# Attention items of a hybrid decoder block: scores before fillers, and splits moved into the last items

## The chip, the cores and the metric

The kernel runs on one core of one Trainium2 chip, as one program that computes a whole decoder layer. The metric is the device time of one execution in microseconds (us). A time is given as the median of several runs; the profile shows one execution.

TensorE (PE) multiplies, VectorE (DVE) and ScalarE (ACT) do the elementwise work and the reductions, GpSimd (POOL) takes some of it, and SyncE (SP) issues nearly all DMAs. Each engine works through its own instructions in order and waits for the others by semaphores.

## The reference

The layer runs an SSD branch and a differential-attention branch in parallel, merges them by gates, and puts a gated feed-forward part behind. The change touches the attention branch and the gate product that is woven into it:

```python
for i in range(seq // Q_BLOCK):                      # 8 blocks of 128 queries
    q0, q1 = i * Q_BLOCK, (i + 1) * Q_BLOCK
    s = jnp.einsum('bhqd,bhkd->bhqk', q[:, :, q0:q1], k[:, :, :q1]) * scale
    p = jax.nn.softmax(jnp.where(mask, s, -jnp.inf), axis=-1)
    p = p.reshape(bsz, DA_HEADS, 2, Q_BLOCK, q1)
    attn = p[:, :, 0] - lam * p[:, :, 1]             # 8 heads, two softmaxes each
    outs.append(jnp.einsum('bhqk,bhkd->bhqd', attn, v[:, :, :q1]))
o = rms_norm(jnp.concatenate(outs, axis=2), subln_w) * (1.0 - lam_init)
...
gate_ssd, gate_att = jnp.split(jax.nn.sigmoid(gates), N_BRANCH, axis=-1)
merged = gate_ssd * (y_ssd @ w_ssd_o) + gate_att * (y_att @ w_attn_o)
```

Everything is float32. The kernel multiplies in a reduced format and keeps the precision by splitting an operand into a high and a low part and adding three products.

## The kernel before, in words

The attention stage works through 64 items, `items[t] = (j, i)`: head `j` of 8, and within it query block `i` of 8, which sees `i + 1` blocks of 128 keys. An item with `i < 4` is short: both softmaxes fit into one PSUM tile, so `scores(t, 0)` does both. With `i >= 4` it is long, and `scores(t, 0)` and `scores(t, 1)` each fill a tile. The score tiles come from `ps_mm`, which has two buffers, so a tile can be written when the exponentials of the tile two before it are done.

For each item: `scores` on PE (L1624, L1625), `maxima` on DVE (mask and row maximum: L1652 and L1653 for short items, L1658 for long ones), `exps` on ACT (L1667 and L1670, with row sums), `probs` on DVE (a reciprocal L1678, a coefficient L1679, and the difference of the two softmaxes L1680), `transposes` on PE with a copy on ACT (L1688, L1689), and `values` on PE (L1699). The work is software-pipelined by hand: the loop turn of item `t` issues scores of `t + 1` and `t + 2`, probabilities of `t + 1`, transposes of `t` and values of `t - 1`. The order on PE, DVE, ACT and POOL is the order in which the code issues; the order on SP is left to a scheduler.

Between these, `fill(n)` puts `n` steps of an independent product on PE: the attention half of the gate weights against the normalised input (`dense_stream`). A step is three matmuls of 512 columns (L1578 to L1580). Eight steps finish one half of a block in PSUM; then a tanh on ACT (L1583) empties the bank into `gev`, and only then can the next step write, since there is one bank. There are 8 x 2 x 8 = 128 steps in all: `NFIRST` ahead of the items, `nfill` spread over the items by `share`, and `NLAST` = 20 behind them, the tail. `fill` carries steps that it does not do over to the next call in `owed`. The splits of the next weight block (`highs` on ACT, L1553; `lows` on DVE, L1550) are handed out one at a time by `one`.

Every four items the outputs of a group are normalised: `norm_o` copies them (ACT, L1706), squares them on POOL (L1707) and returns two closures. `first` sums on DVE and takes the power on POOL (L1710 to L1713, L146), `second` multiplies by the row factor (DVE L1716) and scales the outputs on POOL (L1717). Then `out_o` transposes and writes them to DRAM (`atd`).

These outputs must be read back and split into high and low (`oT`) for the product with `w_attn_o` (`ao`). `att_in` loads half a head into a staging tile `stg` (SP, L1744); `att_split` splits it: the high part on ACT (L101), the low part on DVE (L102), and asks for the next load. There are 14 such parts, two staging tiles of two halves each, four loads asked for at item 56, and the 14 splits stand in the tail beside the 20 fillers. Three DVE sums and five loads for the adaptive norm (`ada_load`, `adas`) stand in the tail too. The tiles come from a list of 43 slots (`Slots`): `get` takes the one that was freed first.

Of the kernel before, what the change touches and what calls it, by code (L numbers as in the profile page):

```python
# [17 lines left out]
P = 128  # L18
D = 1024
S = 1024  # L20
HALF = 512
# [43 lines left out]
def kernel(ctx: ExitStack, tc: tile.TileContext, a: dict, out: bass.AP, dbg=None):  # L65
# [1528 lines left out]
            SP.dma_start(vt[b][:, kt, :], vd[kt][:, j * P : (j + 1) * P])  # L1594

    stream = dense_stream()
    owed = n_step = 0

    def fill(n):
        nonlocal owed, n_step  # L1600
        n, owed = n + owed, 0
        for m in range(n):
            if m and n_step % KD == 0:
                owed = n - m
                return
            next(stream, None)
            n_step += 1

    items = [(j, i) for j in range(8) for i in range(8)]

# [129 lines left out]
    def att_in():  # L1740
        nonlocal n_in
        if n_in < len(parts):
            k, half = parts[n_in]
            SP.dma_start(stg[n_in // 2 % 2][:, n_in % 2, :], atd[k][:, half * HALF : (half + 1) * HALF])  # L1744
            n_in += 1

    def att_split():
        nonlocal n_att
        if n_att < len(parts):
            k, half = parts[n_att]  # L1750
            st = stg[n_att // 2 % 2][:, n_att % 2, :]
            oT[k][half] = new_hl(f"oT{k}_{half}")
            split(oT[k][half][:, 0, :], oT[k][half][:, 1, :], st)
            n_att += 1
            att_in()

# [9 lines left out]
            hi, lo = w_ao[j] = [wp.tile([P, KD, P], F32R, tag=f"w{n}", name=f"wao{j}_{n}", bufs=4) for n in ("hi", "lo")]  # L1766
            split(hi, lo, raw_ao.pop(j))

    NFIRST, NLAST = 6, 20
    nfill = len(blocks) * 2 * KD - NFIRST - NLAST  # L1770
    share = [2, 2, 2, 2, 2, 1, 1, 1]
    load_heads(0)
    done = 0
    with tc.manual_schedule(engines={EN.PE, EN.DVE, EN.Activation, EN.Pool}):
        fill(2)
        scores(0, 0)
        scores(1, 0)
        maxima(0, 0)
        maxima(1, 0)
        exps(0, 0)  # L1780
        exps(1, 0)
        probs(0)
        fill(4)
        norm, pend = [], None
        for t, (j, i) in enumerate(items):
            quota = (j * sum(share) + sum(share[: i + 1])) * nfill // (8 * sum(share)) - done
            done += quota
            f1 = (quota + 1) // 2
            if long_(t + 1):
                scores(t + 1, 1)  # L1790
            fill(f1)
            scores(t + 2, 0)
            fill(quota - f1)
            if long_(t + 1):
                maxima(t + 1, 1)
                exps(t + 1, 1)
            transposes(t, 0)
            if i >= 4:
                transposes(t, 4)
            if t > 0:  # L1800
                values(t - 1)
            maxima(t + 2, 0)
            if i % 4 in (1, 2) and norm:
                norm.pop(0)()
            else:
                one(lows)
            probs(t + 1)
            exps(t + 2, 0)
            if i % 4 == 3 and pend is not None:
                out_o(*pend)  # L1810
                pend = None
            if i % 4 == 0 and t > 0:
                jj, ii = items[t - 1]
                pend = jj, ii // 4
                norm = norm_o(*pend)
            else:
                one(highs)
            if t == 56:
                SL.put(*qst[0], *kst[0], *klo[0], vt[0])
                stg = [SL.get(f"stg{i}", F32, (P, 2, HALF)) for i in range(2)]  # L1820
                for _ in range(4):
                    att_in()
            if j < 7 and i == 1:
                load_heads(j + 1)
        values(len(items) - 1)
        pend = items[-1][0], 1
        norm = norm_o(*pend)
        SL.put(*pts[0], *qst[1], *kst[1], *klo[1], *pts[1], vt[1], *aTs)
        srow2, adas, ada0 = SL.get("srow2"), [SL.get(f"adas{i}") for i in range(5)], n_ada
        for n in range(NLAST):  # L1830
            if n == 4:
                SP.dma_start(srow2, crowd.broadcast_to([P, D]))
            elif n > 4 and n % 2 == 0 and n < 16:
                ada_load()
            if 14 < n < 18:
                ada_sum(False, True)
            if n in (4, 7):
                norm.pop(0)()
            if n == 14:
                out_o(*pend)  # L1840
            if n == 1:
                fetch_ao(0)
            fill(1)
            if n == NLAST - 1:
                fill(0)
            if n < len(parts):
                att_split()
            if n == 13:
                split_ao(0)
        assert n_att == len(parts) and not highs and not lows and n_step == 2 * KD * len(blocks)  # L1850
        SL.put(osb, gev, mstrip, *stg)
        for k in range(KD):
            SL.put(*hT[k])


        mT = [[None] * 2 for _ in range(KD)]
        wo = [[None] * 4 for _ in range(2)]
        fbs = [h * KF + k for k in range(KF) for h in range(2)]

        wsd = [[dp.tile([P, 2, HALF], F32, tag=f"wsd{m}_{i}", name=f"wsd{m}_{i}") for i in range(2)] for m in range(3)]  # L1860

        def early_load(m):
            ra, rb = [SL.get(f"ws{m}_{i}", F32, (P, 2, HALF)) for i in range(2)]
            for r_, b in ((ra, fbs[m]), (rb, NFF + fbs[m])):
                SP.dma_start(r_.rearrange("p h c -> p (h c)"), a["w_up"][b])
            return ra, rb

        def early_sums(m, ra, rb):
            a11, a12, a21, a22 = ra[:, 0], ra[:, 1], rb[:, 0], rb[:, 1]
            V.tensor_tensor(a22, a21, a22, op=ALU.add)  # L1870
            V.tensor_tensor(a21, a11, a21, op=ALU.subtract)
            V.tensor_tensor(a11, a22, a11, op=ALU.subtract)
            V.tensor_tensor(a12, a12, a11, op=ALU.subtract)
            for i, (x_, y_) in enumerate(((a11, a22), (a21, a12))):
                G.dma_start(wsd[m][i][:, 0], x_)
                G.dma_start(wsd[m][i][:, 1], y_)
            SL.put(ra, rb)

        adas += [SL.get(f"adas{i}") for i in range(5, 8)]
        for _ in range(3):  # L1880
            ada_load()
        gth = SL.get("gth2")
        mst = SL.get("mst")
        mt = SL.get("mt")
        fetch_ao(1)
        ws_raw, wo_raw = deque(), deque()

        def wo_load(kp):
            if kp < 4:
                wo_raw.append(SL.get(f"wo1_{kp}_raw", F32, (P, 2, HALF)))  # L1890
                SP.dma_start(wo_raw[-1], a["w_out"][2 * kp * P : (2 * kp + 2) * P, HALF:].rearrange("(k p) c -> p k c", p=P))

        for j in range(KD):
            w = w_ao.pop(j)
            ps = ps_mm(f"ao{j}")
            SP.dma_start(gth, gad[j])
            SP.dma_start(mst, msd[j])
            block_half(ps[:, 0, :], w, oT, 0)
            split_ao(j + 1)
            fetch_ao(j + 2)  # L1900
            if j < 5:
                for _ in range((4, 1, 1, 1, 3)[j]):
                    ada_sum(False, True)
            if j == 0:
                for _ in range(5):
                    ada_load()
            elif j == 4:
                for r in (2, 3):
                    ada_row(r)
                SL.put(srow2, *adas[1:])  # L1910
            elif j == 6:
                ada_turn(3, adas[0][:KD, :P])
                SL.put(adas[0])
            if j < 3:
                ws_raw.append(early_load(j))
            if 0 < j < 4:
                early_sums(j - 1, *ws_raw.popleft())
            if j == 3:
                wo_load(0)
                wo_load(1)  # L1920
            elif j > 3:
                kp = j - 4
                wo[1][kp] = (new_hl(f"wo1_{kp}_hi"), new_hl(f"wo1_{kp}_lo"))
                raw = wo_raw.popleft()
                split(*wo[1][kp], raw)
                SL.put(raw)
                wo_load(kp + 2)
            block_half(ps[:, 1, :], w, oT, 1)
            for half in range(2):
                hsl = slice(half * HALF, (half + 1) * HALF)  # L1930
                V.scalar_tensor_tensor(mt[:, hsl], gth[:, hsl], 1.0, ps[:, half, :], op0=ALU.add, op1=ALU.mult)
                V.tensor_tensor(mt[:, hsl], mt[:, hsl], mst[:, hsl], op=ALU.add)
                mT[j][half] = new_hl(f"mT{j}_{half}")
                split(mT[j][half][:, 0, :], mT[j][half][:, 1, :], mt[:, hsl])
# [729 lines left out]
```

## Time and profile before

| | |
|---|---|
| median of 3 runs | 1814.69 us (1813.57 to 1814.9) |
| the profiled execution, its own time | 1814.9 us |
| its span, first to last instruction | 1813.1 us |
| PE busy | 1766.1 us, 97% |
| DVE busy | 1347.0 us, 74% |
| ACT busy | 918.0 us, 51% |
| POOL busy | 175.9 us, 10% |
| mean granted TensorE clock | 0.997 |
| attention stage, from the first filler to the first `ao` matmul | 697.9 to 993.4 us |

A row of the timeline reads: start, duration, engine, line, operation, output and inputs by name, shapes, count, and in brackets how long the engine had been idle and what ended that. Matmuls are pipelined: a row of 512 columns is shown 0.39 us long, though the next may start much sooner, so pitch is read from start to start. A row of waits reads: who waited for whom, microseconds in all, times, the longest. A row of the stretches reads: from and to, length, then busy time and instruction count of PE, weight load, DVE, ACT and POOL, then the granted clock, the DMA share and GB/s.

### The profile page before, as it was taken

The page shows a single profiled execution, that of the slowest core. Times are in us where ns is not written, and L with a number is a line of the kernel's source. Part 1 is how long each engine was busy: PE and PEld are TensorE (multiplying, and loading weights), DVE is VectorE, ACT ScalarE, POOL GpSimd, SP SyncE. Part 2 cuts the span into 40 slices and gives each one's busy share as a digit, 9 for nine tenths or more (in the row PEclk, how much of TensorE's full clock was granted, in tenths as well). Part 3 has the DMA queues.
Part 4 walks back from the last instruction along what each step waited for, and adds up shares of the span by engine and source line. Part 5 has one row for each costly group of instructions (what it writes and reads, how often), then busy time and mean ns, then how long its engine had stood idle before and what let it go on. Part 6 is the DMA issues. An engine that isn't in the chain of part 4 may idle for free.

```text
span 1813.1 us, 23867 instructions
## 1 busy us (share of the span) xinstructions
PE 1766.1 (97%) x8563; PEld 1459.4 (80%) x8563; DVE 1347.0 (74%) x2048; ACT 918.0 (51%) x1642; POOL 175.9 (10%) x183
## 2 busy tenths in 40 slices
PE   7999999999999999999998999999999999999998
PEld 4788888888778888888886888888888888888887
DVE  7887568865767786778776776679898888875545
ACT  7554345456765313666665132655554544554532
POOL 0000000002551200121121103100000000000001
PEclk9999999999999999999999999999999999999999
DMA  9465643365767798665635879313232223378754
GB/s 375 189 205 165 184 140 104 116 243 171 228 203 250 171 376 224 198 169 143 168 127 177 322 257 376 129 55 122 91 134 105 96 103 110 120 238 295 247 161 158
DMA packets 148330, 337.29 MB, mean 186 GB/s; under 512 B 15570, under 2 KB 50290, under 8 KB 148212
## 3 DMA queue, kind: packets, MB, share of 16 engines
q1 hardware_dynamic: 145012, 325.28, 54.6%
q0 software_dynamic: 3200, 10.49, 1.5%
q8 instruction: 67, 1.10, 0.3%
q14 instruction: 51, 0.42, 0.1%
HBM read 240.46 MB, written 95.25 MB: 185 GB/s over the span
## 4 chain that ended last, share of the span: by engine, by line
PE 48%; DVE 11%; DMA 6%; ACT 4%; issue 3%; POOL 1%; SPq 0%; DVEq 0%; POOLq 0%; ACTq 0%
PE upx L2029 4%; PE upx L2028 4%; PE upx L2030 4%; PE o L1699 2%; DMA gst<-gld_s 2%; PE upy L2029 2%; PE upy L2028 2%; PE upy L2030 2%; PE mix L2102 2%; PE mix L2104 2%; PE mix L2103 2%; PE so L123 2%; PE so L125 2%; PE so L124 2%; PE sc L1625 1%
## 5 line engine op out<-in xcount | busy, mean ns | idle before, releaser
L2028 PE MATMUL upx<-t,wu_t 128*128 128x512 f32 x264 | 103.1, 391 | 0.5 <-DVE cv L2488 0.4
L2029 PE MATMUL upx<-t,wu_t 128*128 128x512 f32 x264 | 102.8, 390 | 0.2 <-DVE t L2159 0.2
L2030 PE MATMUL upx<-t,wu_t 128*128 128x512 f32 x264 | 102.7, 389 | 0.0
L2002 ACT ACTIVATE wu_t<-sab 128x512 fp32r<-128x512 f32 x57 | 34.1, 627 | 127.6 <-DVE sab L2019 127.6
L102 DVE TENSOR_TENSOR g_lo<-gst,g_hi 128x1024 fp32r<-128x1024 f32 (+1 forms) x42 | 47.5, 1134 | 50.5 <-ACT g_hi L101 50.5
L1670 ACT ACTIVATE p<-sc,nmx 128x640 f32<-128x640 f32 (+3 forms) x64 | 61.5, 961 | 36.8 <-DVE nmx L1658 34.2
L1658 DVE CUSTOM_DVE_ANT_0 sc<-sc,mstrip 128x640 f32<-128x640 f32 (+3 forms) x64 | 65.5, 1032 | 13.5 <-PE sc L1625 13.1
L101 ACT ACTIVATE g_hi<-gst 128x1024 fp32r<-128x1024 f32 (+1 forms) x42 | 41.5, 988 | 66.4 <-DMA gst<-gld_s 38.8
L1699 PE MATMUL o<-vt,aT 128*128 128x128 f32 x576 | 74.8, 275 | 0.0
L1699 PEld LDWEIGHTS o<-vt,aT 128*128 128x128 f32 x576 | 69.3, 192 | 0.6
L1624 PE MATMUL sc<-kst,qst 128*128 128x512 f32 (+3 forms) x192 | 67.0, 354 | 0.0
L2547 POOL TENSOR_TENSOR rsf<-rsf,nhalf 128x1 f32<-128x1 f32 x8 | 5.2, 656 | 624.2 <-DVE rsf L2546 624.2
L1689 ACT COPY aT<-at 128x512 f32<-128x512 f32 (+2 forms) x96 | 42.7, 480 | 44.2 <-PE at L1688 44.2
L1625 PE MATMUL sc<-klo,qst 128*128 128x512 f32 (+3 forms) x192 | 64.0, 342 | 0.0
L546 PE MATMUL xx<-xt,xw_t 128*128 128x512 f32 x156 | 60.9, 390 | 0.0
L2046 DVE SCALAR_TENSOR_TENSOR ug<-cg,vec,ug 128x1023 f32<-128x1023 f32 (+1 forms) x44 | 56.3, 1280 | 6.1 <-ACT ug L2045 5.3
L548 PE MATMUL xx<-xt,xw_t 128*128 128x512 f32 x156 | 60.7, 389 | 0.0
L547 PE MATMUL xx<-xt,xw_t 128*128 128x512 f32 x156 | 60.7, 389 | 0.0
L1688 PE MATMUL at<-ident,p 128*128 128x128 f32 x288 | 42.5, 274 | 17.5 <-DVE p L1680 14.2
L2006 DVE TENSOR_TENSOR wu_t<-sab,wu_t 128x512 fp32r<-128x512 f32 x57 | 39.3, 690 | 26.6 <-ACT wu_t L2002 26.6
L2028 PEld LDWEIGHTS upx<-t,wu_t 128*128 128x128 f32 x264 | 49.6, 188 | 11.8 <-DVE cv L2488 1.3
L2029 PEld LDWEIGHTS upx<-t,wu_t 128*128 128x128 f32 x264 | 49.6, 188 | 10.5 <-DVE t L2159 0.5
(579 smaller groups left out, 5728.4 us busy)
## 6 DMA issues: line engine op xcount, KB each, us to landing
adas<-in_w_ada SPq DMA_DIRECT2D x32, 512.0 KB
wuf<-in_w_up SPq DMA_DIRECT2D x22, 512.0 KB
gld_s<-gsum SPq DMA_DIRECT2D x22, 512.0 KB
gst<-gld_s SPq DMA_DIRECT2D x20, 512.0 KB
wdt_raw<-wtd SPq DMA_DIRECT2D x20, 512.0 KB
wuv<-in_w_up SPq DMA_DIRECT2D x19, 512.0 KB
gld_a<-ug SPq DMA_DIRECT2D x33, 256.0 KB
adat<-in_w_ada SPq DMA_DIRECT2D x16, 512.0 KB
```

Of the source, the lines that this page charges most:

```text
L546: T.matmul(o, wh, xh_, start=(k == 0 and first), stop=False, skip_group_check=not first)
L547: T.matmul(o, wh, xl_, start=False, stop=False, skip_group_check=not first)
L548: T.matmul(o, wl, xh_, start=False, stop=(k == KH - 1), skip_group_check=not first)
L1624: T.matmul(sc, qs_[s][:, tsl], ks_[s][:, n0:n1], start=True, stop=False)
L1625: T.matmul(sc, qs_[s][:, tsl], kl[s][:, n0:n1], start=False, stop=True)
L1658: V.tensor_tensor_reduce(out=sc, in0=sc, in1=strip, scale=-1.0, scalar=BIG, op0=ALU.add, op1=ALU.min, accum_out=nmx[bq][s][:, 0:1])
L1670: A.activation(p.rearrange("p (h t) -> p h t", h=2) if i == 4 else p, sc, AF.Exp, scale=-1.0, bias=nmx[bq][s][:, 0:1], accum_out=ssum[bq][ ...
L1699: T.matmul(po_of[j, grp][:, qi, :], aTs[t % 2][:, kt // 4, kt % 4, :], vt[j % 2][:, kt, :], start=(kt == 0), stop=(kt == i))
L2028: T.matmul(out_, wh, xh_, start=(k == 0 and first), stop=False, skip_group_check=not first)
L2029: T.matmul(out_, wh, xl_, start=False, stop=False, skip_group_check=not first)
L2030: T.matmul(out_, wl, xh_, start=False, stop=(k == end), skip_group_check=not first)
L2046: V.scalar_tensor_tensor(u[:, d:], c_[:, : S - d], fw[:, 2 - d : 3 - d], u[:, d:], op0=ALU.mult, op1=ALU.add)
```

## The change

`fill` gets a flag `ended`: once a half of a block is finished, no call does another step until the flag is cleared, which happens once per item (and once per filler of the tail). Before, only the rest of the same call was put off.

If the next item is short, the scores of `t + 2` come first and the whole quota of fillers behind them. Before, half of the quota came first in every item.

`NFIRST` goes from 6 to 8, and `share` gives item 2 of a head one filler less and item 5 one more.

`first` stays ahead of the probabilities at item 5, but goes behind them at item 1; `second` goes behind them at items 2 and 6.

In the turns of items 58 to 63 one split each is done, its low part on POOL. There are three staging tiles, six loads are asked for at item 56, and so eight of the 14 splits are left for the tail. `mstrip`, the mask of the long items, gives back its slot before the tail and not behind it.

```diff
@@ -1594,17 +1594,18 @@
     stream = dense_stream()
-    owed = n_step = 0
+    owed, n_step, ended = 0, 0, False
 
     def fill(n):
-        nonlocal owed, n_step
+        nonlocal owed, n_step, ended
         n, owed = n + owed, 0
         for m in range(n):
-            if m and n_step % KD == 0:
+            if ended:
                 owed = n - m
                 return
             next(stream, None)
             n_step += 1
+            ended = n_step % KD == 0
@@ -1741,16 +1742,18 @@
-            SP.dma_start(stg[n_in // 2 % 2][:, n_in % 2, :], atd[k][:, half * HALF : (half + 1) * HALF])
+            SP.dma_start(stg[n_in // 2 % 3][:, n_in % 2, :], atd[k][:, half * HALF : (half + 1) * HALF])
             n_in += 1
 
-    def att_split():
+    def att_split(eng=V):
         nonlocal n_att
         if n_att < len(parts):
             k, half = parts[n_att]
-            st = stg[n_att // 2 % 2][:, n_att % 2, :]
+            st = stg[n_att // 2 % 3][:, n_att % 2, :]
             oT[k][half] = new_hl(f"oT{k}_{half}")
-            split(oT[k][half][:, 0, :], oT[k][half][:, 1, :], st)
+            o = oT[k][half]
+            A.activation(o[:, 0, :], st, AF.Copy)
+            eng.tensor_tensor(o[:, 1, :], st, o[:, 0, :].bitcast(F32), op=ALU.subtract)
             n_att += 1
             att_in()
@@ -1766,9 +1769,9 @@
-    NFIRST, NLAST = 6, 20
+    NFIRST, NLAST = 8, 20
     nfill = len(blocks) * 2 * KD - NFIRST - NLAST
-    share = [2, 2, 2, 2, 2, 1, 1, 1]
+    share = [2, 2, 1, 2, 2, 2, 1, 1]
@@ -1780,17 +1783,21 @@
-        fill(4)
+        fill(6)
         norm, pend = [], None
         for t, (j, i) in enumerate(items):
             quota = (j * sum(share) + sum(share[: i + 1])) * nfill // (8 * sum(share)) - done
             done += quota
             f1 = (quota + 1) // 2
+            ended = False
             if long_(t + 1):
                 scores(t + 1, 1)
-            fill(f1)
-            scores(t + 2, 0)
-            fill(quota - f1)
+                fill(f1)
+                scores(t + 2, 0)
+                fill(quota - f1)
+            else:
+                scores(t + 2, 0)
+                fill(quota)
@@ -1800,11 +1807,13 @@
             maxima(t + 2, 0)
-            if i % 4 in (1, 2) and norm:
+            if i % 4 in (0, 3):
+                one(lows)
+            elif i == 5:
                 norm.pop(0)()
-            else:
-                one(lows)
             probs(t + 1)
+            if norm and i != 5:
+                norm.pop(0)()
             exps(t + 2, 0)
@@ -1817,15 +1826,17 @@
             if t == 56:
                 SL.put(*qst[0], *kst[0], *klo[0], vt[0])
-                stg = [SL.get(f"stg{i}", F32, (P, 2, HALF)) for i in range(2)]
-                for _ in range(4):
+                stg = [SL.get(f"stg{i}", F32, (P, 2, HALF)) for i in range(3)]
+                for _ in range(6):
                     att_in()
+            if 57 < t:
+                att_split(G)
...
-        SL.put(*pts[0], *qst[1], *kst[1], *klo[1], *pts[1], vt[1], *aTs)
+        SL.put(*pts[0], *qst[1], *kst[1], *klo[1], *pts[1], vt[1], *aTs, mstrip)
...
+            ended = False
             fill(1)
             if n == NLAST - 1:
-                fill(0)
+                while owed:
+                    ended = False
+                    fill(0)
...
-        SL.put(osb, gev, mstrip, *stg)
+        SL.put(osb, gev, *stg)
```

## The prediction

> **What bounds the kernel now.** I read the page's first line, then the busy time by stretch, then the waits inside the attention stretch, then the rows in order of time around them.
>
> ```profile
> span 1813.1 us, 23867 instructions
> ...
> 697.90:970.80 272.90, 253.05 (x1632) 222.84 (x1631) 211.12 (x478) 171.02 (x410) 46.33 (x45) 0.99 0.56 160
> 970.80:993.30 22.50, 16.69 (x67) 13.12 (x66) 14.21 (x23) 12.12 (x20) 3.62 (x3) 0.85 0.75 242
> 993.30:1081.60 88.30, 87.77 (x386) 71.92 (x386) 68.19 (x100) 22.85 (x29) 6.65 (x12) 1.00 0.78 279
> ...
> PE at L1688 <- DVE p L1680: 14.2, 20, 1.3
> PE gap L1578 <- ACT gev L1583: 8.2, 4, 5.1
> PE at L1688 <- ACT ga_hi L1553: 3.3, 3, 1.1
> ```
>
> In the stretches (PE busy first, clock and DMA share near the end) PE is nearly full after 993.3, but lacks 20 us in the items and 6 us in the 20-filler tail, where the mean clock is 0.85. So PE sets the end, and what it waits for in these two stretches is what the change can win. The waits name it: 17.5 us in 23 waits at the transposes (the three charged to ACT stand at the same place and have the same length), 8.2 us at a filler that needs its PSUM bank emptied by the tanh (L1583).
>
> A pass 512 wide starts 0.23 us after the one before (below, 993.12 and 993.35), so I measure a loss from start to start; it is about 0.16 longer than the wait printed. By that measure each head loses 2.78 us: 0.51 at the 7-wide transposes (A), 1.27 at the 8-wide (B), 1.0 at the 3-wide one of the next head (C).
>
> ```profile
> 824.40 0.39 PE L1625 MATMUL sc<-klo,qst 128*128 128x512 f32 x1
> 824.94 1.23 DVE L1658 CUSTOM_DVE_ANT_0 sc<-sc,mstrip 128x1024 f32<-128x1024 f32 x1 [0.42 <-PE sc L1625]
> 828.93 0.95 PE L1688 MATMUL at<-ident,p 128*128 128x128 f32 x7 [0.35 <-DVE p L1680]
> 830.08 1.11 ACT L1670 ACTIVATE p<-sc,nmx 128x1024 f32<-128x1024 f32 x1 [1.26 <-DVE nmx L1658]
> 830.98 1.04 POOL L1717 TENSOR_TENSOR osb<-osb,sqt 128x512 f32<-128x512 f32 x1 [2.58 <-DVE sqt L1716]
> 831.52 0.52 DVE L1679 SCALAR_TENSOR_TENSOR coef<-ssum,nlam,rsm 128x1 f32<-128x1 f32 x1
> 833.50 0.74 PE L1688 MATMUL at<-ident,p 128*128 128x128 f32 x5 [1.11 <-DVE p L1680]
> ...
> 841.09 0.39 PE L1625 MATMUL sc<-klo,qst 128*128 128x512 f32 x1
> 843.12 0.68 DVE L1710 TENSOR_REDUCE sso<-osb 128x4 f32<-128x512 f32 x1
> 844.18 0.16 DVE L1678 RECIPROCAL rsm<-ssum 128x2 f32<-128x2 f32 x1
> 845.19 0.82 DVE L1658 CUSTOM_DVE_ANT_0 sc<-sc,mstrip 128x640 f32<-128x640 f32 x1
> 845.42 0.52 PE L1688 MATMUL at<-ident,p 128*128 128x128 f32 x3 [0.85 <-DVE p L1680]
> 845.93 0.15 DVE L1716 TENSOR_TENSOR sqt<-sqt,rsm 128x4 f32<-128x4 f32 x1
> 846.20 1.10 DVE L1679 SCALAR_TENSOR_TENSOR coef<-ssum,nlam,rsm 128x1 f32<-128x1 f32 x1
> 846.40 0.80 ACT L1670 ACTIVATE p<-sc,nmx 128x640 f32<-128x640 f32 x1
> 847.50 0.39 PE L1624 MATMUL sc<-kst,qst 128*128 128x512 f32 x1
> ```
>
> The first group is one chain: PE ends item 7's first scores at 824.63, DVE runs without a break through maximum, `first`, probabilities of item 6, the next maximum; ACT takes the exponential, DVE the last probabilities, PE goes on at 833.50: 8.87 us. PE's own work in between is 8.87 less A and B, 7.09.
>
> **The change part by part.** *Shares and the place of `norm`.* Item 5 of a head gets a second filler, item 2 loses one. Three passes are 3 x 0.2275 = 0.68 us, and at item 5 the second filler stands behind the scores that start the chain: PE's work becomes 7.77. The chain gets shorter by 0.30: `second` now stands behind the probabilities, so L1717 on POOL no longer runs beside L1679, which took 0.52 there and 1.10 at 846.20 and ended with it. A is gone, B keeps 8.57 - 7.77 = 0.80: a gain of 0.98 a head. Putting item 7's scores ahead of its filler costs nothing as long as item 7's exponential (830.08 + 1.11 = 831.19) leaves the bank first. PE, which began that item at 830.98, will come 0.68 - 0.51 later, at 831.15: a tie, worth 0.1 at most if lost.
>
> *Scores first where the next item is short.* From the end of item 3's scores (841.32) PE has two fillers and one, as before one and two; PE's arrival at the 3-wide transposes hardly moves against the chain. `first` (843.12 to the next reciprocal at 844.18, 1.06 us) now comes after the probabilities, so 0.85 of waiting vanishes. What is late next: `first` still stands ahead of item 4's maximum, that maximum ends at 845.93, its exponential can start some 0.2 later (here 846.40, behind a copy of transposes that were late) and takes 0.80, and the next scores (here 847.50) need that PSUM bank. PE would arrive at 841.32 + 5.07 (four fillers 2.73, scores 0.59 twice, transposes and values 1.16) = 846.39, and waits to 846.95. Of C's 1.0 I count 0.45.
>
> ```profile
> 961.96 0.96 PE L1688 MATMUL at<-ident,p 128*128 128x128 f32 x7 [0.75 <-DVE p L1680]
> 966.23 1.06 PE L1688 MATMUL at<-ident,p 128*128 128x128 f32 x8 [1.28 <-DVE p L1680]
> ```
>
> The last head has no scores ahead and only the extra filler helps: 0.68. With the three small waits for tanh (0.68 together, removed by `ended`) the items give 7 x 0.98 + 0.68 + 7 x 0.45 + 0.68 = **11.4**. Ends: the 21.9 that all losses add up to, and 3, if DVE's chain swallows nearly all.
>
> *Start: eight fillers ahead, so that the first half ends there; `ended`.*
>
> ```profile
> 707.69 0.59 ACT L1583 ACTIVATE gev<-gap 128x512 f32<-128x512 f32 x1
> 708.34 0.50 PE L1578 MATMUL gap<-b,w_gate_hi 128*128 128x512 f32 x1 [2.12 <-ACT gev L1583]
> 709.98 0.63 PE L1579 MATMUL gap<-b,w_gate_hi 128*128 128x512 f32 x1
> 713.12 0.49 PE L1688 MATMUL at<-ident,p 128*128 128x128 f32 x3
> ```
>
> PE stands 2.12 + 0.16 us for a tanh that ACT takes late. Then its passes are slow: from 709.98 to 713.12 it needs 3.14 us for five passes of 512 and four of 320, which at 0.23 and 0.15 are 1.7; with the edges some 1.6 is lost. Both go: 3.9. In their place I put 0.15 (tanh against one set of scores) and 0.45 for a wait as in C, which this head did not have: **3.3**; ends 1.5 and 3.9. [...]
>
> *Six splits inside the last items, third staging tile.*
>
> ```profile
> 974.52 0.50 PE L1578 MATMUL gap<-hT,ga_hi 128*128 128x512 f32 x1 [0.69 <-ACT gev L1583]
> 982.84 1.16 ACT L101 ACTIVATE oT<-stg 128x512 fp32r<-128x512 f32 x2 [1.41 <-DMA stg<-atd]
> 984.75 0.58 ACT L1583 ACTIVATE gev<-gap 128x512 f32<-128x512 f32 x1
> 985.38 0.80 PE L1578 MATMUL gap<-b,ga_hi 128*128 128x512 f32 x1 [5.12 <-ACT gev L1583]
> 988.86 1.29 ACT L101 ACTIVATE oT<-stg 128x512 fp32r<-128x512 f32 x2 [1.83 <-DMA stg<-atd]
> 989.68 0.40 PE L1580 MATMUL gap<-b,ga_lo 128*128 128x512 f32 x1
> 993.12 0.39 PE L1580 MATMUL gap<-hT,ga_lo 128*128 128x512 f32 x1
> 993.35 0.39 PE L123 MATMUL ao<-oT,wao_hi 128*128 128x512 f32 x1
> ```
>
> In the tail PE's twelfth filler is done at 980.1, but its tanh is queued on ACT behind splits that wait for staged loads: 5.12 + 0.16 lost; from 985.38 to 989.68 it then needs 4.3 us for eight passes and four transposes of 128, about 2.3: 2.0 more. With eight splits left, six of them loaded long before, ACT is through by about 978, and the second bank costs what the first costs now, 0.69 + 0.15: 5.28 + 2.0 - 0.84 = **6.4**; ends 4 and 7.
>
> ```profile
> L101 ACT ACTIVATE oT<-stg 128x512 fp32r<-128x512 f32 x14 | 8.5, 628 | 8.5 <-DMA stg<-atd 7.7 <-DMA ws<-in_w_up 0.7
> L1707 POOL TENSOR_TENSOR osb<-osb 128x512 f32<-128x512 f32 x16 | 16.7, 1041 | 167.6 <-ACT osb L1706 167.6
> ...
> 926.85 1.91 SPq L561 DMA_DIRECT2D adas<-in_w_ada  x4
> ```
>
> The six splits cost 0.63 us each on ACT, behind an exponential whose successor still waits for DVE (the 1.26 idle at 830.08 covers 0.63), and about 1.04 each on POOL, idle there; uncovered they would cost 3.8 on ACT. POOL's subtraction runs while DVE takes maxima from PSUM and should be over before the next L1679; if each caught one as at 846.20, 6 x 0.88 = 5.3. [...] On SP the staged loads move ahead of the tail; the five `adas` loads, four of them at 926.85 to 928.8 now, lose their tiles to the early splits and must wait for those of items 61 to 63, behind 962. They are read by DVE after the fifteenth tail filler, some 20 us later, and land where ten staged loads were: nothing.
>
> *Afterwards.* PE hardly waits from 993.3 on, so all of it should carry to the end; the next stretch, at a DMA share of 0.78, gets it 6 us sooner and may give back up to 5. I take nothing.
>
> **Sum.** 11.4 + 3.3 + 6.4 = 21.1 against the profiled execution's own 1814.9 us (span 1813.1 and 1.8 around it; the runs' median is 0.2 below): **1793.8**.
>
> **The rivals.**
> - *DVE binds the items.* Its 211 us in 273 look free, but in items 5 and 6 its chain has no gap and PE only waits elsewhere. Then the items give 3 and the time is 1814.9 - 3 - 9.7 = 1802.2. Against it: A and B shrink by arithmetic alone. 15%.
> - *All waits vanish*, the chains having slack that I don't see: 21.9 + 3.3 + 6.4 gives 1783.3. Against it the bank wait at item 4. 10%.
> - *The next stretch gives back 5*, DMA being the limit there: 1799. For it the 279 GB/s, against it that PE waits there 0.5 us in all now. 12%.
> - *Slower: ACT waits for staged loads inside the items.* The queue is in order; a split whose load is late holds the exponentials, DVE and PE. In the tail splits waited up to 1.83 us (before 988.86); at 2.5 us for each of the six, with slow passes worth 2.0 after each, 6 x 4.5 = 27 is lost, more than the 21.1 gained: 1821. It decides from about 1.5 us each, if slow passes follow. Against it: the six loads are asked for two items before the first split, some 8 us. 4%.
> - *It does nothing*: the waits only move to the bank and tanh, about 1814. 4%.
>
> The forecast itself holds 55%. From these the range is 1786 to 1804: the ends of the three terms and two rivals. What a measurement here can tell from no change is about 0.2%, 3.6 us: faster 92%, within 4%, slower 4%.
>
> **What would show it.** No wait at the 7-wide transposes, about 0.65 printed at the 8-wide, none at the 3-wide but some 0.4 at scores L1624 for ACT's L1670; L1679 at 0.22 in every item; no filler wait over 1 us, none at 708; the tail about 16 us long at full clock. Wrong would be: waits of DVE's p as long as before, L1679 or L1680 stretched beside POOL in the last head, ACT waiting for `stg` there, or new PE waits behind the tail.

## The result and the profile after

The changed kernel takes 1796.24 us (median of 4 runs, 1794.83 to 1798.24), the kernel before beside it 1814.13 us (4 runs). The ratio is 0.9902 with a 95% interval of 0.9885 to 0.9919: about 18 us faster, where 21 were forecast. The profiled execution took 1795.55 us.

In the changed kernel the lines from L1624 on stand one further down: scores are L1625 and L1626, long maxima L1659, long exponentials L1671, coefficient L1680, probabilities L1681, transposes L1689, `second` L1717 and L1718, the splits of the outputs L1755 and L1756.

The page's first line, then the stretches (items, tail, and what follows; the columns are those of the table before), then the waits inside the attention stage:

```profile
span 1793.8 us, 23879 instructions
```

```profile
699.40:959.40 260.00, 252.68 (x1634) 221.08 (x1632) 204.11 (x478) 173.42 (x416) 52.75 (x50) 1.00 0.61 171
959.40:975.50 16.10, 14.73 (x66) 11.55 (x66) 11.40 (x19) 8.75 (x15) 5.62 (x4) 1.00 0.81 293
975.50:1063.80 88.30, 88.30 (x391) 73.00 (x391) 68.21 (x100) 23.84 (x30) 7.22 (x13) 1.00 0.82 288
```

```profile
PE at L1689 <- DVE sqt L1717: 4.1, 8, 1.3
...
PE sc L1625 <- ACT p L1671: 2.6, 6, 0.5
...
PE gap L1578 <- ACT gev L1583: 1.4, 2, 0.7
```

PE now lacks 7 us in the items (20 before) and 1.4 in the tail (6 before), and the tail runs at full clock (1.00, 0.85 before). 14.2 and 3.3 us of waiting at the transposes have become 4.1, in 8 waits, one for each head, and one wait of 0.3 that is charged to the probabilities. The releaser named there, L1717, is only DVE's last small instruction; the probabilities, L1681, stand right ahead of it. In their place stands a wait that was not there: 2.6 us at scores, for the exponential that holds the PSUM bank. The stage is 19.32 us shorter (from the first filler to the first `ao` matmul, 295.43 before, 276.11 now), and the span 19.3. Behind the stage nothing was given back: the rest took 819.75 us before and takes 818.25 now, while the part ahead of the stage, which the change does not touch, took 697.92 and takes 699.43.

Rows of the timeline of the changed kernel, in order of time: in one head the bank wait at item 4 and the chain of item 7, then the last head, and the tail.

```profile
904.36 0.50 PE L1625 MATMUL sc<-kst,qst 128*128 128x512 f32 x1 [0.45 <-ACT p L1671]
...
913.93 0.39 PE L1626 MATMUL sc<-klo,qst 128*128 128x512 f32 x1
...
918.23 1.23 DVE L1659 CUSTOM_DVE_ANT_0 sc<-sc,mstrip 128x1024 f32<-128x1024 f32 x1
...
919.61 1.11 ACT L1671 ACTIVATE p<-sc,nmx 128x1024 f32<-128x1024 f32 x1 [2.09 <-DVE nmx L1659]
...
921.04 0.22 DVE L1680 SCALAR_TENSOR_TENSOR coef<-ssum,nlam,rsm 128x1 f32<-128x1 f32 x1
...
922.73 1.06 PE L1689 MATMUL at<-ident,p 128*128 128x128 f32 x8 [0.43 <-DVE sqt L1717]
...
954.76 1.06 PE L1689 MATMUL at<-ident,p 128*128 128x128 f32 x8 [1.28 <-DVE sqt L1717]
...
959.37 0.48 PE L1578 MATMUL gap<-hT,ga_hi 128*128 128x512 f32 x1
...
963.05 0.50 PE L1578 MATMUL gap<-hT,ga_hi 128*128 128x512 f32 x1 [0.69 <-ACT gev L1583]
...
969.47 0.50 PE L1578 MATMUL gap<-b,ga_hi 128*128 128x512 f32 x1 [0.69 <-ACT gev L1583]
...
975.54 0.39 PE L123 MATMUL ao<-oT,wao_hi 128*128 128x512 f32 x1
```

From the end of the first scores of item 7 by pitch (913.93 + 0.23 = 914.16) to its transposes at 922.73 the chain takes 8.57 us; 0.59 of it PE stands, 0.43 as printed. From 959.37 to 975.54 the tail takes 16.17 us, against 22.51 before.

### The profile page after: what moved, and what is told of

Its sections match the earlier page's. It is cut to its first block, busy times and chain, and to the rows that moved or that the text cites. A ratio compares the mean times of both kernels' runs of the same rounds, so it can differ in the third digit from the quotient of the medians.

```text
span 1793.8 us, 23879 instructions
## 1 busy us (share of the span) xinstructions
PE 1763.5 (98%) x8563; PEld 1456.3 (81%) x8563; DVE 1335.8 (74%) x2042; ACT 916.9 (51%) x1642; POOL 184.5 (10%) x189
## 4 chain that ended last, share of the span: by engine, by line
PE 56%; DVE 8%; DMA 3%; ACT 2%; issue 2%; POOL 1%; SPq 1%; DVEq 0%; POOLq 0%; ACTq 0%
PE upx L2043 4%; PE upx L2042 4%; PE upx L2044 4%; PE o L1700 2%; PE upy L2043 2%; PE upy L2042 2%; PE upy L2044 2%; PE dx L2438 2%; PE dx L2439 2%; PE dx L2437 2%; PE dy L2438 2%; PE dy L2437 2%; PE dy L2439 2%; PE mix L2116 2%; PE mix L2117 2%
## 5 line engine op out<-in xcount | busy, mean ns | idle before, releaser
L1659 DVE CUSTOM_DVE_ANT_0 sc<-sc,mstrip 128x640 f32<-128x640 f32 (+3 forms) x64 | 65.9, 1029 | 14.4 <-PE sc L1626 13.9
L1671 ACT ACTIVATE p<-sc,nmx 128x640 f32<-128x640 f32 (+3 forms) x64 | 61.6, 962 | 28.3 <-DVE nmx L1659 24.6
L1625 PE MATMUL sc<-kst,qst 128*128 128x512 f32 (+3 forms) x192 | 70.7, 373 | 2.9 <-ACT p L1671 2.6
L1626 PE MATMUL sc<-klo,qst 128*128 128x512 f32 (+3 forms) x192 | 63.8, 341 | 0.0
L521 ACT ACTIVATE xw_t<-xsab 128x512 fp32r<-128x512 f32 x39 | 23.7, 627 | 67.5 <-DVE xsab L530 66.9
```

What stands on the lines that cost most here:

```text
L1625: T.matmul(sc, qs_[s][:, tsl], ks_[s][:, n0:n1], start=True, stop=False)
L1626: T.matmul(sc, qs_[s][:, tsl], kl[s][:, n0:n1], start=False, stop=True)
L1659: V.tensor_tensor_reduce(out=sc, in0=sc, in1=strip, scale=-1.0, scalar=BIG, op0=ALU.add, op1=ALU.min, accum_out=nmx[bq][s][:, 0:1])
L1671: A.activation(p.rearrange("p (h t) -> p h t", h=2) if i == 4 else p, sc, AF.Exp, scale=-1.0, bias=nmx[bq][s][:, 0:1], accum_out=ssum[bq][ ...
```

## The experiments

Stage stands for the time from the first filler to the first `ao` matmul in the profiled execution. Ratios are to the kernel before, run beside each of them.

| kernel | median us | ratio, 95% interval | stage us |
|---|---|---|---|
| before | 1814.13 | 1 | 295.43 |
| changed | 1796.24 | 0.9902 [0.9885, 0.9919] | 276.11 |
| e1_splits_alone | 1809.21 | 0.9971 [0.9959, 0.9982] | 287.66 |
| e2_order_undone | 1802.91 | 0.9935 [0.9922, 0.9947] | 282.51 |
| e3_norm_undone | 1800.59 | 0.9921 [0.9908, 0.9935] | 281.19 |
| e4_share_undone | 1796.46 | 0.9897 [0.9882, 0.9912] | 275.94 |
| e5_first6 | 1795.00 | 0.9899 [0.9886, 0.9913] | 275.17 |
| e6_ended_undone | 1795.84 | 0.9902 [0.9889, 0.9916] | 276.02 |
| e7_first6_ended_undone | 1795.91 | 0.9904 [0.9891, 0.9918] | 275.30 |
| e8_split_dve | 1799.02 | 0.9922 [0.9908, 0.9935] | 279.08 |
| v1_norm_later | 1802.62 | 0.9933 [0.9919, 0.9947] | 283.67 |
| v2_two_banks | 1800.95 | 0.9927 [0.9914, 0.9939] | 281.64 |
| v3_banks_alone | 1793.58 | 0.9889 [0.9873, 0.9905] | 273.96 |
| v4_norm_later_out_early | 1807.47 | 0.9962 [0.9949, 0.9975] | 286.98 |

**The splits alone.** The kernel before, with six splits in the last items and nothing else of the change:

```diff
+            if 57 < t:
+                att_split(G)
```

> The kernel before, with nothing of the change but the six splits inside the last items (three staging tiles, low part on POOL, mstrip's slot given back early). Theory (three parts that add up: start 3.6, items 9.4, tail 6.3 us): the 5.28 us loss at the second tanh of the tail and its slow passes go, the rest stays: about 1807.8 us, tail 16.2 us long, waits at the transposes as before. Rival (the tail's gain needs the other parts, because ACT in the last items is too full): the splits hold up exponentials there, 1811 or more.

It gained 7.8 us in the stage and about 5 in the median; its profiled execution was the fastest of its six. In the stage 6.3 of the gain are the tail, 16.19 us long instead of 22.51. Nearly all the rest lies at the start. In the tail the second wait for the tanh is 0.69 us instead of 5.12. The wait of 2.12 us at the start and those at the transposes stayed. What differs at the start stands in the next two rows, the window of this kernel and the matching one of the kernel before, which issue the same work there (the clock is the third column from the end):

```profile
705.00:714.00 9.00, 6.88 (x40) 5.58 (x39) 7.46 (x17) 6.01 (x16) 0.00 (x0) 1.00 0.88 247
```

```profile
705.00:714.00 9.00, 6.88 (x31) 5.51 (x30) 6.51 (x15) 4.78 (x13) 0.00 (x0) 0.81 0.91 242
```

PE is idle for as long in both, but here 40 matmuls pass in the 9 us at full clock, there 31 at 0.81. The slow passes behind the start's wait, of which the prediction took 1.6 us, came in one execution and not in the other; what decides between the two, these rows do not show.

**The order undone.** The changed kernel, with half of the fillers first in every item again:

```diff
-            if long_(t + 1):
-                scores(t + 1, 1)
-                fill(f1)
-                scores(t + 2, 0)
-                fill(quota - f1)
-            else:
-                scores(t + 2, 0)
-                fill(quota)
+            if long_(t + 1):
+                scores(t + 1, 1)
+            fill(f1)
+            scores(t + 2, 0)
+            fill(quota - f1)
```

> The changed kernel, but half the fillers come ahead of the scores again when the next item is short. Theory (a chain from item 3's scores): one filler less stands between those scores and the 3-wide transposes, so PE waits there about 0.5 us again and still about 0.4 for the bank at item 5's scores; 0.45 a head more, about 1799. Rival (the order is what the change lives on): the waits at the 3-wide transposes come back whole, 1.0 a head or more, 1803 or above.

The stage became 6.4 us longer. These are rows of its timeline, at the start and in one head:

```profile
708.17 0.50 PE L1578 MATMUL gap<-b,w_gate_hi 128*128 128x512 f32 x1 [0.69 <-ACT gev L1583]
...
843.58 0.52 PE L1689 MATMUL at<-ident,p 128*128 128x128 f32 x3 [0.46 <-DVE p L1681]
...
846.33 0.50 PE L1625 MATMUL sc<-kst,qst 128*128 128x512 f32 x1 [0.51 <-ACT p L1671]
...
864.89 1.06 PE L1689 MATMUL at<-ident,p 128*128 128x128 f32 x8 [0.65 <-DVE sqt L1717]
```

The 3-wide wait is back beside the bank wait, and the 8-wide one is 0.80 by pitch, not 0.59. By pitch the 3-wide wait is 0.62 in most heads. The kinds are those of the theory; that the start loses 0.84 and 0.83 too, and the 8-wide 0.2, it had not counted. In time it stands at the rival's 1803, but not by the rival's mechanism.

**The place of `norm` undone.** `first` at items 1 and 5 and `second` at items 2 and 6 ahead of the probabilities again:

```diff
-            if i % 4 in (0, 3):
-                one(lows)
-            elif i == 5:
+            if i % 4 in (1, 2) and norm:
                 norm.pop(0)()
+            else:
+                one(lows)
             probs(t + 1)
-            if norm and i != 5:
-                norm.pop(0)()
```

> The changed kernel, but first and second stand ahead of the probabilities again, as before. Theory: at the 3-wide transposes PE waits 0.85 us and not at the bank behind it; at the 8-wide 0.3 more, because L1717 on POOL again stretches L1679 to 0.52; together 0.7 a head, about 1801. Rival (norm's place is worth nothing once the order and the shares are changed): within 1 us of 1796.2, L1679 stretched but hidden.

5.1 us in the stage, as the theory said; the rival falls. The coefficient, an instruction on one column, is long again in 14 of 64 items, 0.45 to 1.10 us, as many as in the kernel before, and it ends with POOL's scaling. The timeline:

```profile
875.46 0.52 PE L1689 MATMUL at<-ident,p 128*128 128x128 f32 x3 [0.84 <-DVE p L1681]
...
876.24 1.10 DVE L1680 SCALAR_TENSOR_TENSOR coef<-ssum,nlam,rsm 128x1 f32<-128x1 f32 x1
...
876.28 1.04 POOL L1718 TENSOR_TENSOR osb<-osb,sqt 128x512 f32<-128x512 f32 x1 [0.82 <-DVE rsm L1679]
```

876.24 + 1.10 is 877.34, and 876.28 + 1.04 is 877.32. In the changed kernel one of 64 coefficients is longer than 0.25 us (0.72).

**The shares undone.** `share = [2, 2, 2, 2, 2, 1, 1, 1]` in the changed kernel.

> The changed kernel with the old shares (item 2 two fillers, item 5 one). Theory: the waits at the 7-wide and 8-wide transposes together are 0.68 longer a head, but the wait for the bank at item 5's scores (0.6) goes, because a filler more stands ahead of it; in the last head 0.68 is lost; about 1797.5. Rival (the shares remove most of the waits, as the prediction had it with 0.98 a head): 7 us, 1803.

Nothing: the median moved by 0.2 us, within what can be measured, and the stage by -0.2. In its timeline the 7-wide wait is back and the bank wait has gone:

```profile
854.67 0.52 PE L1689 MATMUL at<-ident,p 128*128 128x128 f32 x3 [0.35 <-DVE p L1681]
...
858.95 1.06 PE L1689 MATMUL at<-ident,p 128*128 128x128 f32 x8 [0.43 <-DVE sqt L1717]
```

(The view ends inside the 7-wide group, so its row counts 3 of 7 transposes.) By pitch these are 0.51 and 0.60, with another 0.27 at the scores between them. The changed kernel has 0.59 at the 8-wide and about 0.59 at the bank. With the passes that start late beside each wait, both come to about 1.6 a head. The filler that fills the 7-wide wait at item 5 is taken from item 2, and then it is missing one turn later, where PE reaches the bank too early.

**Six fillers ahead, and the old rule for a finished half.** Three kernels: `NFIRST = 6` alone, the old condition in `fill` alone, and both.

```diff
-    NFIRST, NLAST = 8, 20
+    NFIRST, NLAST = 6, 20
...
-        fill(6)
+        fill(4)
```

```diff
-            if ended:
+            if m and n_step % KD == 0:
...
-            ended = n_step % KD == 0
```

> The changed kernel with six fillers ahead of the items instead of eight (102 spread over them), the flag ended kept. Theory (the flag alone is enough: it puts the ninth step into the next item, so the tanh has time): no wait over 0.5 us at a filler near the start, within 1 us of 1796.2. Rival (eight fillers are needed so that the half ends ahead of the items): the 2.12 us wait is back, 1798.5 or more.

> The changed kernel with the old stopping rule in fill (only the rest of the same call is put off), eight fillers kept. Theory (eight fillers alone are enough for the start; elsewhere a second call in the same item costs a wait of a few tenths, as the three before): waits for the tanh of 0.5 to 1.0 us in all inside the items, 1796.5 to 1797.5. Rival (the flag removes long waits): waits of 2 us at a filler, 1800 or more.

> The changed kernel with both undone: six fillers ahead and the old stopping rule. Theory: only together do they bring back the wait of 2.12 us at the first filler of the second half, 2.3 by pitch; whether slow passes follow depends on the execution (they did in the profiled run before, not in that of the splits alone): 1799 without, 1800.5 with them. Rival (either one is enough to bring it back): this run then differs from one of the two others by less than 1 us.

All three stand within 1.3 us of the changed kernel, and the third refutes what I had in mind for the first two. The timeline of the kernel with both undone, where the kernel before waits 2.12 us:

```profile
708.11 0.40 PE L1578 MATMUL gap<-hT,w_gate_hi 128*128 128x512 f32 x1
...
708.98 0.41 PE L1688 MATMUL at<-ident,p 128*128 128x128 f32 x2
...
709.73 0.59 ACT L1583 ACTIVATE gev<-gap 128x512 f32<-128x512 f32 x1
...
710.38 0.50 PE L1578 MATMUL gap<-b,w_gate_hi 128*128 128x512 f32 x1 [0.15 <-ACT gev L1583]
```

The eighth filler, at 708.11, ends the half; the ninth comes a whole item later and waits 0.15. With scores first, an item's fillers are one call. The old rule puts off the rest of a call in which a half ends, so it now catches the ninth, which before stood in a second call behind the scores. So of these three parts the order alone is enough to take the start's wait away. Without it, eight fillers ahead and the flag together still leave 0.84 and 0.83 (the second kernel above).

**The low parts of the six splits on DVE.** `att_split(V)` in the items.

> The changed kernel with the low part of the six early splits on DVE instead of POOL. Theory (DVE sets the pace in the last items, and its queue stands still until ACT has done the high part, which comes behind an exponential): the maxima of items 61 to 63 start 1 to 2 us later and PE waits for probabilities there; 3 us more, about 1799. Rival (POOL's subtraction collides with DVE's instructions of two SBUF inputs and costs as much): within 0.5 us of 1796.2 or faster.

2.8 us in the median and 3.0 in the stage. The timeline of the last items:

```profile
944.75 0.50 PE L1625 MATMUL sc<-kst,qst 128*128 128x512 f32 x1 [0.61 <-ACT p L1671]
...
947.38 1.10 DVE L1756 TENSOR_TENSOR oT<-stg,oT 128x512 fp32r<-128x512 f32 x1 [0.79 <-ACT oT L1755]
...
950.79 0.50 PE L1625 MATMUL sc<-kst,qst 128*128 128x512 f32 x1 [0.76 <-ACT p L1671]
...
953.43 0.95 PE L1689 MATMUL at<-ident,p 128*128 128x128 f32 x7 [0.75 <-DVE p L1681]
...
958.30 1.06 PE L1689 MATMUL at<-ident,p 128*128 128x128 f32 x8 [1.88 <-DVE sqt L1717]
```

The waits of the last head are 0.5 to 0.9 longer than in the changed kernel (by pitch 0.77 against 0.29 at the scores at 944.75, 0.91 against none at those at 950.79, 0.91 against 0.23 at the 7-wide, 2.03 against 1.44 at the 8-wide). In the last head, then, work added to DVE's chain costs PE time, and POOL is the better place for this work.

**The norm steps an item later.** An attempt to take what was left: `first` behind the probabilities at items 2 and 6, `second` behind the maxima at items 3 and 7, `out_o` in the next item. The second kernel puts one half of the last block of fillers into the other PSUM bank as well.

```diff
+            if i % 4 == 3 and norm:
+                norm.pop(0)()
             if i % 4 in (0, 3):
                 one(lows)
-            elif i == 5:
-                norm.pop(0)()
             probs(t + 1)
-            if norm and i != 5:
+            if i % 4 == 2 and norm:
                 norm.pop(0)()
             exps(t + 2, 0)
-            if i % 4 == 3 and pend is not None:
+            if (i % 4 == 0 or t == len(items) - 1) and pend is not None:
                 out_o(*pend)
```

```diff
-                ps = ps_wa(f"gap{j}_{half}", 0)
+                ps = ps_wa(f"gap{j}_{half}", int(j == 7 and half == 0))
```

> The changed kernel with the two norm steps of an ended half and the PSUM copy of its output placed one item later than the changed kernel has them (first step behind the second probs pass of a short item, second step behind the maxima, output later). In the changed kernel's stage the PE stands 0.59 us a head at the eight-wide transposes, 0.59 at the scores that wait for the exps of the 1024-wide row, and 1.44 at the last head. Theory: these waits come from DVE work (the norm copy and square, 1.0 us and 0.3 us) that stands ahead of the maxima and the probs in the two waits' items; moved to the items where DVE has slack, they go: 7 x (0.6 + 0.45) and about 1.0 at the last head, 8 us, so 1787 to 1789. Rival: the chain score, maxima, exps, probs has itself no slack left and the waits only change their place (to the transposes of another item or to the output's transpose), 1793 to 1797.

> The kernel of v1_norm_later, with the first half of the last tail block accumulated in the other PSUM bank of that pool than the half before. In the changed kernel the PE stands 0.84 us twice in the tail at a filler's first matmul for the tanh of the filler ahead. Theory: both waits are for the bank; with another bank for one half one of them goes, 0.8 us below v1 (1786 to 1788), and if the next half finds its bank free too, 1.7 below. Rival: the wait passes to the next half, or the tanh chain sets the tail's end in any case: within 0.3 us of v1.

The first missed by 14 us. The 8-wide wait did shrink, from 0.59 to 0.33 by pitch in most heads, and the bank wait mostly went. But the timeline shows this at item 2 of a head:

```profile
873.02 1.04 POOL L1708 TENSOR_TENSOR osb<-osb 128x512 f32<-128x512 f32 x1 [6.21 <-DMA atd<-osb]
...
873.10 1.37 DVE L1681 SCALAR_TENSOR_TENSOR p<-p,coef,p 128x384 f32<-128x384 f32 x1
...
874.62 0.52 PE L1689 MATMUL at<-ident,p 128*128 128x128 f32 x3 [0.51 <-DVE p L1681]
```

The square of the next group writes the half of `osb` from which the output's DMA reads, and waits for it, 6.21 us here. It starts 0.08 ahead of the probabilities, and these take 1.37 us, where the changed kernel's take 0.62. The output's transposes wait as well (0.15 to 1.2 a group, 2.08 in the tail), and in three heads so do the scores of item 4's turn, 0.5 to 1.4 for an exponential. In all the stage is 7.6 us longer than the changed kernel's.

In the second kernel both tail waits of 0.84 are gone, and the stage is 2.0 shorter than in the first.

**The two parts of that apart.** The bank alone in the changed kernel; and the later norm steps with the output where the changed kernel has it, and the bank.

> The changed kernel, and nothing else than the other PSUM bank for the first half of the last tail block (the one line in which the kernel with both differed from the one with later norm steps; there both tail waits of 0.84 us went and the time fell by 1.7 us). Theory: the two tail waits of the changed kernel (0.84 us each) are for the bank and have nothing to do with the norm steps, so they go here too: 1.7 us below the changed kernel's 1796.2, so 1793.8 to 1795. Rival: in the changed kernel's order the tanh or the splits set the end of the tail, and the time stays within 0.4 us of 1796.2.

> The norm steps as in v1_norm_later, the output's transposes where the changed kernel has them, and the two banks. Theory: what v1 lost came from the later output. Its activation result stands in the half of osb that the next square writes, so a later output's DMA held the square on POOL back (it waited for that DMA in 11 of 16 halves) until it ran beside the 384-wide probs, which took 1.38 instead of 0.62 us (and the 3-wide transposes then stood 0.66), and the copies of the output fell ahead of the transposes' own. With the output early, the probs of 384 take 0.62 again, the waits at the three-wide and at the output go, and of the eight-wide wait 0.33 or less stays: 1788 to 1791. Rival: the norm steps cost DVE the same time in the new place, so the waits at transposes come back elsewhere, or the output's transposes now wait for POOL's scaling: at or above the other kernel of this job, 1794 to 1800.

The bank alone: 1793.58, the best of all these kernels. In its stage, 2.15 us shorter than the changed kernel's, no filler of the tail waits, and from 960.33 to 974.53 the tail takes 14.20 us, 1.97 less. The two intervals of the ratio overlap, so the runs alone would not prove it; the trace shows the place.

The other kernel, 1807.47, is the rival's case, and beyond it. The timeline at the same place of a head:

```profile
866.87 0.68 DVE L1550 TENSOR_TENSOR ga_lo<-ga_raw,ga_hi 128x512 fp32r<-128x512 f32 x1
867.10 1.35 POOL L1718 TENSOR_TENSOR osb<-osb,sqt 128x512 f32<-128x512 f32 x1 [0.34 <-DVE sqt L1717]
...
867.66 0.80 DVE L1680 SCALAR_TENSOR_TENSOR coef<-ssum,nlam,rsm 128x1 f32<-128x1 f32 x1
...
868.50 0.66 PE L1725 MATMUL ot<-ident,osb 128*128 128x128 f32 x4 [1.20 <-POOL osb L1718]
...
876.16 0.62 DVE L1681 SCALAR_TENSOR_TENSOR p<-p,coef,p 128x384 f32<-128x384 f32 x1
```

The 384-wide probabilities take 0.62 again and the 3-wide wait is gone, as the theory had it; the 8-wide keeps 0.33. But the output's transposes now wait for POOL's scaling, 1.03 to 1.95 by pitch, twice a head. `second` a whole item before the output, as in the changed kernel, keeps PE from that; its price is that 0.59 and not 0.33 stands at the 8-wide transposes.

## Why the prediction was right, point by point

Forecast 1793.8, measured 1796.24: 21.1 us of gain were counted, and 19.35 came in the profiled executions (1814.9 to 1795.55). Between the medians it is 17.9; the profiled execution of before is the slowest of its four.

In both kernels the stage has the same 1697 PE rows. Taken from start to start, with the usual pitch for each kind of pass (0.227 us for 512 columns, 0.11 for a transpose), they stand for 257.6 us of work in both. What goes beyond that, 37.86 us before and 18.54 now, is the loss, and it can be added up item by item.

- **Tail: 6.4 forecast, 22.51 - 16.17 = 6.34 measured.** One tanh wait of 5.12 became 0.69, the passes behind it run at full clock (1.00 in the tail, 0.85 before), and the tail is 16 us long. The split alone showed the same wait falling.
- **Start: 3.3 forecast; by its own measure 3.6.** The 3-wide transposes of item 2 came 15.20 us after the first filler with 11 fillers done, and come 12.28 us after it (711.71) with 12 done; with 0.68 for the extra filler that is 3.6. Two reasons in this step were wrong. It is the order that takes the wait away; the eight fillers and the flag without it leave most of the loss. And 1.6 us of it were slow passes, which one execution had (clock 0.81 from 705 to 714) and another did not (1.00): without them this term would have been 2, so that the size came out is in part luck.
- **Items: 11.4 forecast, the rest of the 19.32, 9.4, measured.** This is the term that was too large.
  - *The chain of item 7* takes 8.57 us, as forecast to the hundredth, and it does so within 0.02 in all eight heads. PE's work in it is 7.98 and not 7.77, so the residue is 0.59 and not 0.80. With the old order it is 0.80. The chain sets the time, so this does not change the sum: items 6 and 7 of seven heads lost 12.9 us and lose 6.0, a gain of 6.9 where 7 x 0.98 was forecast.
  - *The shares* were given 0.68 a head. Without them the kernel is no slower. In the step the arithmetic at items 5 to 7 holds, but the filler taken from item 2 has no price there. The forecast does pay it, in another term: the 0.55 at the bank, counted in C against the order, goes when the shares are undone. So the sum was nearly right here, and what it said of the cause was not.
  - *C*: 3.15 forecast, 2.5 measured (items 2 to 4 of seven heads). The 3-wide wait is gone in six of seven heads; in the seventh 0.42 is left, behind the one coefficient that still ran beside POOL and took 0.72. At the bank of item 4 0.59 stands, 0.55 forecast. But the passes beside that wait start late too, and together they cost 0.73 to 0.81 in each of six heads.
  - *The last head* was to gain 0.68 and gained 0.14. Its 7-wide wait went from 0.91 to 0.23 and the 1.44 at the 8-wide stayed, but 0.55 came at the scores of item 5. The first head loses about as much at the same place, and with 0.18 more at its item 3 that is 0.7 which no term had.
  - *The three small tanh waits*: 0.68 forecast. Two gave 0.6; the third stood right ahead of a 3-wide wait and is counted in C.

Rows of the changed kernel show what came at item 5 of the last head:

```profile
941.97 0.60 ACT L1583 ACTIVATE gev<-gap 128x512 f32<-128x512 f32 x1 [1.37 <-PE gap L1580]
942.47 0.90 ACT L1671 ACTIVATE p<-sc,nmx 128x768 f32<-128x768 f32 x1
...
943.51 0.50 PE L1625 MATMUL sc<-kst,qst 128*128 128x512 f32 x1
```

A half of a block ends in item 4 there. Its tanh is ahead of the exponential on ACT, and ACT stands 1.37 us until the eighth filler is done; the scores need the bank that the exponential holds. The loss moves with that tanh: it is in the first and the last head here, in the sixth head with the shares undone, and in the third and the last with six fillers ahead. With it, the parts add up to the 9.4 measured.

- **The norm's place**: of 14 stretched coefficients one is left, where none was forecast, and to put the steps back costs 5.1 us of the stage.
- **Afterwards: nothing forecast, nothing lost.** PE is busy for all of the 88.3 us behind the tail, at a DMA share of 0.82 instead of 0.78. That rival, with 12%, fell. So did that of ACT waiting for staged loads: no split in the items waits for one (the only such wait, 1.44 us, is in the tail), and no coefficient of the last head is longer than 0.25 us beside POOL's part of the splits, though that takes 1.3 us each and not 1.04.

The rival in which DVE binds the items was partly true: 4.1 us of waits for DVE stay. The two attempts to move its norm steps did not get them: each brought waits elsewhere that cost more.

## What to carry to other kernels

Order a shared engine's work by the chain that others wait for: scores that start a chain go ahead of work that only fills, and a rule that puts off a filler must see all the fillers of an item (here one call for them was enough, and the new flag added nothing to it). When a wait goes, look for the next resource on the same path (here the PSUM bank two tiles on) and count the gain only up to it; a filler moved from one item to another is paid for where it is missing. Look at what runs beside a small instruction and not only at its size: here the coefficient on one column took 1.10 us instead of 0.22 beside POOL's scaling (846.20 before), while the long maximum, which reads PSUM, took 1.23 in the changed kernel beside POOL's split (950.26) and without it. So POOL's large operations belonged beside such maxima, or where DVE waits.

## What the runs showed of the hardware

- An idle PE of about 2.3 us was followed by slow passes in one execution (clock 0.81 over 9 us) and by none in another (1.00), at the same place of the program. The later waits of 2.03 to 2.09 by pitch, with the low parts on DVE and with the later norm steps, had none either (clock 1.00 in the windows around them).
- The coefficient and the probabilities, DVE operations with two or more SBUF inputs, took 0.75 to 0.88 us longer in these three places, where a POOL operation on 128x512 began within 0.1 us of them: a coefficient on one column 1.10 instead of 0.22 (846.20 before), the probabilities on 384 columns 1.37 instead of 0.62 (873.10 with the later norm steps), those on 896 columns 1.97 instead of 1.15 (824.88 in the same kernel). Twice, with POOL 0.06 and 0.07 us behind it, the coefficient kept its 0.22 (918.34 with later norm steps and two banks, 906.14 with the later norm steps alone). A coefficient that began later beside POOL (831.52 against 830.98 before) took only 0.52. The reciprocal, with one input, took 0.15 to 0.17 beside POOL and alone.
- Where a DVE split was first, it was POOL's scaling that took longer. In the rows of the last experiment its scaling began 0.23 after the weight split of L1550, took 1.35 instead of 1.04, and ended 0.90 after that split. In five more heads of that kernel it began 0.16 to 0.24 after one, took 1.35 to 1.42, and ended 0.90 after it too. The coefficient that began in its middle ended with it (867.10 + 1.35 and 867.66 + 0.80). Where only a coefficient began in its middle, the scaling took 1.04.
